# Two pads of 64 bytes that move every large on-chip tile of an encoder block from byte 64 to byte 0 modulo 128

## The chip, the cores and the metric

The kernel runs on one core of one Trainium2 chip. The metric is the device time of one execution in microseconds; of the kernel before, three runs are given, and their median counts.

## The reference, cut to what matters

One block of a streaming encoder works on x of 512 x 1024 in fp32. One input projection feeds two attention branches and their gates; each branch is projected, gated and summed, and an output projection and a layer norm follow. A gated MLP with a causal convolution of width 3 and a second layer norm end the block.

```
proj = x @ w_in                              # 1024 -> q/k/v of two branches, indexer, two gates
y_a  = top-k attention with a relative bias  # 8 heads of 64
y_s  = stick-breaking attention              # 8 heads of 64
merged = sigmoid(g_a + b_a) * (y_a @ w_branch_dsa) + sigmoid(g_b + b_b) * (y_s @ w_branch_sb)
x = layer_norm(alpha * x + merged @ w_out)
u, g = split(x @ w_ffn_in)                   # 1024 -> 2 x 2816
h = gelu(causal_dwconv(u, conv_w, conv_b)) * g
x = layer_norm(alpha * x + h @ w_ffn_out)    # 2816 -> 1024
```

## The kernel before, in words

Every product of fp32 operands is made of three matmuls (type fp32r): each operand is split into a high part, which ScalarE (ACT) writes with a copy, and a low part, which VectorE (DVE) or GpSimd (POOL) gets by subtracting the high part. The three are high x high, high x low and low x high. In the input projection (L233 to L235, and L270 to L272 for the values), the branch projections (L611 to L613, L817 to L819), the output projection (L866 to L868) and the MLP (L937 to L939, and L1017 to L1019 for its second half) the moving operand has 512 columns in most matmuls, 384 or 256 in some, and the stationary one is a 128 x 128 block. The second MLP product follows a Strassen scheme, with sums of weight blocks and of hidden blocks made on the way.

A stream object (class `Stream`) brings the weights in pieces of 128 x 1024: a DMA on the queue of SyncE (SP) fills a `raw` tile, L104 makes `whi` of it, L113 makes `wlo`, or for some pieces a negated copy (L107) and an accumulating DMA (L110) do. Three `raw`, three `whi` and three `wlo` buffers turn over. Attention heads run one after the other on ACT, DVE and POOL, and the list `FILL` names projections whose matmuls TensorE (PE) runs in between, a few at a time. The weights of the sticks or of the softmax are turned over for the last product of a head, by PE for the first heads (L452) and, for the later ones, by a pair of 16-bit DMA transposes from `own`, a view into the tile `bm` or `keep`, to `pl` (L478); `weigh` (L511) multiplies them with the values, and reads 128-column pieces with a gap between them, up to three in one matmul.

Where the tiles lie is set by pools. The pool `cst` opens first on the left side of SBUF (on-chip memory, 229,376 bytes in each of 128 partitions), behind 16,512 bytes that the program reserves. Its five tiles are one after the other, each taken up to a multiple of 32 bytes: `ident` (512 bytes in a partition), `mhalf` (4), `bgt` (16 fp32, the gate biases), `cwt` (22 x 4 fp32, the taps and biases of the convolution) and `wi` (24 fp32, padded to 32). The pools `rawp`, `ring`, `bp` and later `cp`, `tp`, `ep`, `fp`, `hp`, `rp` stand behind it on the left. On the right side the pool `edge` opens first, ending at byte 229,344, with one tile `rb` of 8 fp32; `xp`, and later `dp`, `qp`, `wp`, grow from it towards the left. All other small tiles go through the helper `padded`, which allots the free size rounded up to 32 fp32 and returns the part that was asked for:

```
def padded(pool, shape, dt=F32, **kw):
    n = int(np.prod(shape[1:]))
    t = pool.tile([shape[0], -(-n // 32) * 32], dt, **kw)[:, :n]
    return t if len(shape) == 2 else t.rearrange("p (a b) -> p a b", a=shape[1])
```

So every tile that lies behind `cst` or before `edge` has a size that is a multiple of 128 bytes, and all of them have one residue modulo 128: 64 on both sides. The first `raw` tile is at byte 17,600, the pool `bp` begins at 54,464, `x1h` is at 170,688, `xh` at 155,584. Of the tiles larger than 4 bytes in a partition `ident` alone begins at byte 0 modulo 128, at 16,512.

`bgt` is read as a per-partition bias, one column at a time, by the gates' activations (L639, L645, L799), and is filled by one DMA; `rb` is written on L669 and L670 and read by two small matmuls on L674.

Of the kernel before, what the change touches and what calls it, by code (L numbers as in the profile page):

```python
# [11 lines left out]
F32 = mybir.dt.float32  # L12
F32R = mybir.dt.float32r
# [8 lines left out]
H = 8  # L22
# [105 lines left out]
def tile_block(ctx: ExitStack, tc: tile.TileContext, xT, xN, w_qi, w_ki, w_t, w_v, w_br, w_o, w_fi, w_fo,  # L128
# [10 lines left out]
# [6 lines that stand above are left out]
    cst = ctx.enter_context(tc.tile_pool(name="cst", bufs=1))  # L145
    edge = ctx.enter_context(tc.tile_pool(name="edge", bufs=1, side="right"))
# [73 lines left out]
    nc.gpsimd.memset(mhalf, -0.5)  # L220
    nc.scalar.activation(mhalf, mhalf, AF.Sigmoid)
    nc.gpsimd.memset(mhalf, -0.5)
    bgt = cst.tile([128, 16], F32, name="bgt")
    cwt = cst.tile([128, FC, 4], F32, name="cwt")


# [437 lines left out]
    idx_keys()  # L664

    oh = bp.tile([64, NREL], F32R, tag="beta", bufs=2, name="oh")
    rb = edge.tile([64, H], F32R, name="rb")
    nc.gpsimd.tensor_copy(oh, ohf)
    nc.vector.tensor_copy(rb[0:32], rbf)  # L669
    nc.vector.tensor_sub(rb[32:64], rbf, r32(rb[0:32]))  # L670
# [628 lines left out]
```

## Time and profile before

| | |
|---|---|
| Time, median of 3 runs | 746.8 us (746.47 to 747.76) |
| Profiled execution, first to last instruction | 744.9 us, granted TensorE clock 0.998 |
| PE busy | 735.6 us, 99% |
| DVE busy | 572.0 us, 77% |
| ACT busy | 408.0 us, 55% |
| POOL busy | 148.8 us, 20% |
| DMA traffic | 117.03 MB |

The profiled execution gives its span, and no time of its own beside it: the span lies 1.9 us below the median of the runs, and that is taken as what lies around it.

Engines are PE (TensorE's matmuls), PEld (its weight loads), DVE, ACT, POOL and SP; an engine's name with a q is its instruction queue. "L104" is a line of the kernel. A group's row gives line, engine, operation, output<-inputs by the program's names, the tile's shape, the count, the total of busy us and the mean ns of one, and then the idle time in front of them. A row of the timeline gives start and length in us. Matmuls are pipelined, and the trace gives each its whole passage, so that rows of 0.39 us start every 0.23 us: the step from start to start is what a matmul costs.

### The profile page before, as it was taken

The page shows a single profiled execution, that of the slowest core. Times are in us where ns is not written, and L with a number is a line of the kernel's source. Part 1 is how long each engine was busy: PE and PEld are TensorE (multiplying, and loading weights), DVE is VectorE, ACT ScalarE, POOL GpSimd, SP SyncE. Part 2 cuts the span into 40 slices and gives each one's busy share as a digit, 9 for nine tenths or more (in the row PEclk, how much of TensorE's full clock was granted, in tenths as well). Part 3 has the DMA queues.
Part 4 walks back from the last instruction along what each step waited for, and adds up shares of the span by engine and source line. Part 5 has one row for each costly group of instructions (what it writes and reads, how often), then busy time and mean ns, then how long its engine had stood idle before and what let it go on. Part 6 is the DMA issues. An engine that isn't in the chain of part 4 may idle for free.

```text
span 744.9 us, 9755 instructions
## 1 busy us (share of the span) xinstructions
PE 735.6 (99%) x3477; PEld 616.9 (83%) x3477; DVE 572.0 (77%) x907; ACT 408.0 (55%) x572; POOL 148.8 (20%) x161
## 2 busy tenths in 40 slices
PE   9999999999999999999999999999999999999995
PEld 7888888888888888888889888888888888888885
DVE  5569888999679898668755866686767668668985
ACT  6466867797785587845473533443444344345430
POOL 0002224365743332000101111011101101110011
PEclk9999999999999999999999999999999999999999
DMA  7445887796476455527832544444443444448632
GB/s 266 157 128 188 207 172 173 158 214 163 116 181 154 135 126 136 131 85 247 289 57 86 170 141 142 141 143 143 141 166 114 161 136 149 144 140 268 202 130 84
DMA packets 73631, 117.03 MB, mean 157 GB/s; under 512 B 42536, under 2 KB 42792, under 8 KB 73584
## 3 DMA queue, kind: packets, MB, share of 16 engines
q1 hardware_dynamic: 66304, 93.98, 42.0%
q0 software_dynamic: 5744, 18.38, 9.9%
q10 hardware_dynamic: 1536, 4.06, 2.1%
q8 instruction: 27, 0.44, 0.3%
q14 instruction: 20, 0.16, 0.1%
HBM read 95.93 MB, written 9.98 MB: 142 GB/s over the span
## 4 chain that ended last, share of the span: by engine, by line
PE 89%; DVE 3%; POOL 2%; issue 2%; DMA 2%; ACT 2%; DVEq 0%; POOLq 0%; ACTq 0%
PE u_ps L937 5%; PE u_ps L939 5%; PE g_ps L937 5%; PE u_ps L938 5%; PE g_ps L939 5%; PE g_ps L938 5%; PE m L1019 2%; PE m L1017 2%; PE m L1018 2%; PE av_ps L511 2%; PE ga_ps L234 2%; PE ga_ps L233 2%; PE gb_ps L235 2%; PE gb_ps L234 2%; PE ga_ps L235 2%; PE gb_ps L233 2%
## 5 line engine op out<-in xcount | busy, mean ns | idle before, releaser
L104 ACT ACTIVATE whi<-raw 128x1024 fp32r<-128x1024 f32 (+1 forms) x124 | 123.8, 1001 | 143.1 <-PE g_ps L938 43.7
L113 DVE TENSOR_TENSOR wlo<-raw,whi 128x1024 fp32r<-128x1024 f32 (+1 forms) x105 | 123.9, 1181 | 36.3 <-ACT whi L104 35.6
L939 PE MATMUL u_ps<-x1h,wlo 128*128 128x512 f32 (+1 forms) x192 | 71.4, 372 | 0.0
L937 PE MATMUL u_ps<-x1h,whi 128*128 128x512 f32 (+1 forms) x192 | 71.3, 372 | 0.0
L938 PE MATMUL u_ps<-x1l,whi 128*128 128x512 f32 (+1 forms) x192 | 71.3, 371 | 0.0
L937 PE MATMUL g_ps<-x1h,whi 128*128 128x512 f32 (+1 forms) x184 | 69.9, 380 | 0.0
L938 PE MATMUL g_ps<-x1l,whi 128*128 128x512 f32 (+1 forms) x184 | 69.9, 380 | 0.0
L939 PE MATMUL g_ps<-x1h,wlo 128*128 128x512 f32 (+1 forms) x184 | 69.9, 380 | 0.0
L939 PEld LDWEIGHTS u_ps<-x1h,wlo 128*128 128x128 f32 x192 | 36.2, 188 | 6.3
L938 PEld LDWEIGHTS u_ps<-x1l,whi 128*128 128x128 f32 x192 | 36.2, 188 | 6.3
L937 PEld LDWEIGHTS u_ps<-x1h,whi 128*128 128x128 f32 x192 | 36.2, 188 | 6.2
L939 PEld LDWEIGHTS g_ps<-x1h,wlo 128*128 128x128 f32 x184 | 34.6, 188 | 6.6
L938 PEld LDWEIGHTS g_ps<-x1l,whi 128*128 128x128 f32 x184 | 34.6, 188 | 6.5
L937 PEld LDWEIGHTS g_ps<-x1h,whi 128*128 128x128 f32 x184 | 34.6, 188 | 6.5
L960 DVE TENSOR_TENSOR t<-raw 128x512 f32<-128x512 f32 x11 | 7.6, 693 | 40.1 <-DMA raw<-in_w_fo_dram 39.2
L569 POOL TENSOR_TENSOR bm<-win,score 128x256 f32<-128x256 f32 (+2 forms) x24 | 26.9, 1147 | 32.2 <-DMA pl<-bm 27.3
L985 ACT ACTIVATE c<-c,cwt 128x512 f32<-128x512 f32 x22 | 15.9, 725 | 27.5 <-DVE c L984 27.3
L979 POOL MEMSET u<- 128x2 f32 x22 | 2.1, 98 | 143.7 <-ACT whi L104 99.2
L993 DVE TENSOR_TENSOR hF<-g_ps,c 128x512 f32<-128x512 f32 x22 | 15.1, 687 | 19.7 <-PE g_ps L939 19.7
L835 POOL TENSOR_TENSOR rstd<-rstd,mhalf 128x1 f32<-128x1 f32 x8 | 7.7, 959 | 104.6 <-DVE rstd L834 104.6
L423 DVE MAX8 m<-score 128x8 f32<-128x256 f32 (+2 forms) x48 | 26.6, 556 | 0.9
L557 POOL TENSOR_TENSOR beta<-beta,keep 128x1280 f32<-128x1280 f32 x8 | 21.6, 2704 | 26.7 <-DVE keep L554 26.7
(576 smaller groups left out, 2088.3 us busy)
## 6 DMA issues: line engine op xcount, KB each, us to landing
raw<-in_w_fi_dram SPq DMA_DIRECT2D x44, 512.0 KB, 3.3
raw<-in_w_t_dram SPq DMA_DIRECT2D x32, 512.0 KB, 3.7
raw<-in_w_fo_dram SPq DMA_DIRECT2D x26, 512.0 KB, 4.2
wlo<-in_w_t_dram POOLq DMA_DIRECT2D x14, 512.0 KB, 5.8
raw<-in_w_br_dram SPq DMA_DIRECT2D x8, 512.0 KB, 4.0
raw<-in_w_o_dram SPq DMA_DIRECT2D x8, 512.0 KB, 4.1
raw<-in_w_v_dram SPq DMA_DIRECT2D x7, 512.0 KB, 4.6
raw_b<-in_w_fo_dram SPq DMA_DIRECT2D x6, 512.0 KB, 5.5
```

Of the source, the lines that this page charges most:

```text
L104: self.high = nc.scalar.activation(hi[:, :w], t[:, :w], AF.Copy).ins
L113: self.done[key] = eng.tensor_sub(lo[:, :w], t[:, :w], r32(hi[:, :w])).ins
L233: nc.tensor.matmul(ps[:M], wh[:, c], xh[k], start=(k == 0), stop=False)
L234: nc.tensor.matmul(ps[:M], wh[:, c], xl[k], start=False, stop=False)
L235: nc.tensor.matmul(ps[:M], wl[:, c], xh[k], start=False, stop=(k == KC - 1))
L423: nc.vector.max(m8, sc)
L557: nc.gpsimd.tensor_mul(beta, beta, keep[:, 1:ATT + 1])
L569: nc.gpsimd.tensor_add(bm[:, OFF[j]:OFF[j] + N], win[:, 512 - N:512], score[j])
L937: nc.tensor.matmul(ps[:, c], wh[:, kc], x1h[:, k, c], start=(k == 0), stop=False)
L938: nc.tensor.matmul(ps[:, c], wh[:, kc], x1l[:, k, c], start=False, stop=False)
L939: nc.tensor.matmul(ps[:, c], wl[:, kc], x1h[:, k, c], start=False, stop=(k == KC - 1))
L985: nc.scalar.activation(c, c, AF.Gelu_apprx_tanh, bias=cwt[:, f, 3:4])
```

## The change

```
-    bgt = cst.tile([128, 16], F32, name="bgt")
+    bgt = padded(cst, [128, 16], name="bgt")
...
-    rb = edge.tile([64, H], F32R, name="rb")
+    rb = edge.tile([64, 3 * H], F32R, name="rb")[:, :H]
```

`bgt` takes 128 bytes of a partition in place of 64, and `rb` takes 96 in place of 32; the columns that are used, and every instruction's operands apart from their addresses, stay. On the left, `cwt` moves from byte 96 to byte 32 modulo 128, and `wi` and everything behind it moves up by 64 bytes, the first `raw` tile to 17,664 (138 x 128). On the right everything before `rb` moves down by 64, `x1h` to 170,624 (1333 x 128). The narrowest space between a left and a right tile of one time, 256 bytes between `hp` and `qp`, becomes 128; no pair of tiles comes to share a byte that did not share one before.

## The prediction

> **What bounds the kernel now.** I read the page's first part, the chain that ended last, the busy time by stage, and then the starts of single matmuls.
>
> ```profile
> span 744.9 us, 9755 instructions
> PE 735.6 (99%) x3477; PEld 616.9 (83%) x3477; DVE 572.0 (77%) x907; ACT 408.0 (55%) x572; POOL 148.8 (20%) x161
> ...
> PE 89%; DVE 3%; POOL 2%; issue 2%; DMA 2%; ACT 2%; DVEq 0%; POOLq 0%; ACTq 0%
> ```
>
> The kernel is one stream of matmuls, and 89% of the chain is PE. The stages say where PE is whole (us, then busy us and instructions of each engine):
>
> ```profile
> 4.50:45.00 40.50, 40.23 (x200) 34.17 (x200) 24.31 (x36) 21.47 (x34) 0.71 (x1) 1.00 0.60 198
> 45.00:190.00 145.00, 145.00 (x706) 122.67 (x707) 130.54 (x265) 109.76 (x177) 56.79 (x44) 1.00 0.76 177
> 190.00:255.00 65.00, 64.66 (x307) 53.96 (x306) 53.93 (x89) 43.92 (x69) 30.33 (x26) 1.00 0.59 145
> 255.00:400.00 145.00, 145.00 (x709) 122.98 (x708) 111.08 (x176) 93.00 (x124) 17.18 (x21) 1.00 0.52 151
> 400.00:676.00 276.00, 276.00 (x1255) 230.06 (x1255) 194.69 (x259) 114.80 (x143) 35.91 (x53) 1.00 0.43 143
> 676.00:733.00 57.00, 57.00 (x267) 47.77 (x266) 48.50 (x67) 22.60 (x26) 4.17 (x6) 1.00 0.56 185
> ```
>
> PE shows no idle time to speak of, but its rows overlap and can cover small gaps, so I take what a matmul costs from start to start. First the chain in the MLP:
>
> ```profile
> 449.02 0.45 PE Q L1019 x2
> ...
> 474.86 0.45 PE Q L1019 x2
> ```
>
> Between these two stand one round of two hidden blocks: 2 x 48 matmuls of L937 to L939 and 18 of L1017 to L1019, 114 of 512 columns in 25.84 us, 226.67 ns each. Then 256 and 384 columns, from the timeline and the chain:
>
> ```profile
> 399.82 0.28 PE L939 MATMUL u_ps<-x1h,wlo 128*128 128x256 f32 x1
> ...
> 402.94 0.28 PE L937 MATMUL u_ps<-x1h,whi 128*128 128x256 f32 x1
> ```
>
> ```profile
> 10.16 0.52 PE qi_ps L312 x3
> ```
>
> With the 25 rows between, 26 steps of 256 columns take 3.12 us, 120.0 ns each; 384 columns take 0.52/3 = 173.3. The three lie on one line: 106.67 ns per 256 columns, and 13.33 ns a matmul on top. Those 13.33 ns are as long as 32 columns, and 32 columns of fp32 are 128 bytes. That is the one number in the profile that could speak for the change, so most of what follows is about it.
>
> Over the whole stream the columns (2847 matmuls of 512, 290 of 256, 200 of 384, 137 of 128, 3 of 8, counted in the trace) and 13.33 ns for each of the 3477 come to 723.8 us. The first start and the last are these:
>
> ```profile
> 1.20 2.99 PE L210 MATMUL idle_ps<-idle 128*128 128x512 bf16 x7 [1.20 <-DVE idle L207]
> ```
>
> ```profile
> 737.10 0.28 PE L1019 MATMUL m<-whi,bl 128*128 128x256 f32 x1
> ```
>
> That is 735.9 us, so 12.1 us are stalls: by the same subtraction 1.7 in the warm-up matmuls, 1.1 to 45 us, 4.5 to 190, 2.4 to 255, 2.1 to 320, and 0.4 in all the rest. Behind the last start lie 7.8 us of the last block's norm and output. Whatever does not change the 13.33 ns can win at most the 10 us of stalls behind the warm-up and a part of the 7.8.
>
> **The change part by part.** No instruction is added, removed or moved; no wait is added, since no pair of tiles comes to overlap that did not, and nothing is moved past a queue. The DMA that fills `bgt` and the copies into `rb` have the same shapes. What remains is the address, and it reaches three kinds of work.
>
> *Matmuls.* If a misaligned start made the 13.33 ns, each misaligned start should cost. `weigh` offers the test: its first moving operand is three runs of 128 columns with gaps, each run beginning at byte 64 modulo 128, and the same count of columns stands in one run elsewhere.
>
> ```profile
> 283.86 0.34 PE L511 MATMUL av_ps<-pth,va 128*128 128x384 f32 x1
> 284.04 0.34 PE L511 MATMUL av_ps<-ptl,va 128*128 128x384 f32 x1
> 284.21 0.22 PE L511 MATMUL av_ps<-pth,va 128*128 128x128 f32 x1
> ```
>
> Two matmuls of three runs take 0.35 us, 175 ns each, beside 173.3 for one run. Two more starts at byte 64 cost 1.7 ns, 0.8 each, which is within the 10 ns to which the rows are given; by the theory they would cost 26.7. The second witness is the warm-up row above: its moving tile, of bf16, is at 54,464, byte 64 modulo 128 too, and 7 matmuls take 2.99 us, 427 ns each. At half the column rate found above, 512 columns are 426.7 ns, and nothing is left for a start. So the 13.33 ns belong to the fp32 matmul, not to its address, as far as these rows reach. I take 0. Both ends for the range, from the nearest row: 0.8 ns on each of 3477 starts, 2.9 us less or more.
>
> [...]
>
> *DVE, ACT and POOL.* The convolution reads the same tile at offsets of 4 and 8 bytes, and the norm reads tiles at their beginning; output, width and operation agree.
>
> ```profile
> L983 DVE SCALAR_TENSOR_TENSOR c<-u,cwt,c x22: 743/750/1401, 406.8 to 670.1; 128x512 f32<-128x512 f32 x22
> ```
>
> ```profile
> L984 DVE SCALAR_TENSOR_TENSOR c<-u,cwt,c x22: 739/752/753, 408.6 to 671.9; 128x512 f32<-128x512 f32 x22
> ```
>
> ```profile
> L839 DVE SCALAR_TENSOR_TENSOR r<-r,mv,ln 128x512 f32<-128x512 f32 x14 | 9.8, 746 | 0.0
> ...
> L980 ACT ACTIVATE u<-u_ps 128x512 f32<-128x512 f32 x22 | 12.8, 581 | 0.0
> L1155 ACT ACTIVATE m<-P 128x512 f32<-128x512 f32 x2 | 1.1, 583 | 0.0
> ```
>
> Offsets 4, 8 and 0 give 750, 752 and 746 ns; on ACT a copy from PSUM to offset 8 takes 581 and one to offset 0 takes 583. An engine's time moves by 0.8% at most with the address. I take 0; DVE, ACT and POOL carry 7% of the chain, 52 us, so the bound is 0.4 us either way. Where these engines lie beside PE, its matmuls cover them: 130.5 us of DVE against 145.0 of PE in the tightest stage, and DVE would have to slow by 11% to lose that cover.
>
> *DMA.* All weight loads now land at another byte of a row. In a stretch that is DMA alone (355 to 360 us):
>
> ```profile
> DMA packets 580, 2.08 MB, mean 416 GB/s; under 512 B 72, under 2 KB 72, under 8 KB 580
> ...
> q1 hardware_dynamic: 559, 2.03, 100.2%
> ```
>
> The queue moves 2.03 MB, 496 packets of 4 KB, in 100.2% of 16 x 5 us: 162 ns a packet, 10.1 for 256 bytes. [...]
>
> *The sum.* 0 for PE, 0 for the engines, -0.1 for DMA: the profiled execution stays at 744.8, and with the 1.9 us between span and median the time is 746.7 us. A difference under 0.2%, 1.5 us, cannot be told from no change here: the three runs spread over 1.3 us.
>
> **The rivals.**
>
> *Faster, by PE:* the beginning of a moving operand is fetched only when the matmul before has ended, a 128-byte piece at a time, and a start in its middle wastes half or all of the 13.33 ns; later runs are fetched ahead, so that the three-run row is blind to it. For it: 13.33 ns is just 128 bytes. Against: the bf16 row, and 175 beside 173.3. Price: behind 255 us PE is alone, and 2231 matmuls (709, 1255 and the 267 of the last stretch) save 29.7 us; of the 1213 before, 16.2 us, DVE's 130.5 of 145 us leaves perhaps half. Together 38, so 709 us if all of it goes, 728 if half.
>
> [...] The transposes move packets of 256 bytes from `own`, which goes from byte 192 to byte 0 modulo 256. In one of them:
>
> ```profile
> DMA packets 2489, 0.62 MB, mean 175 GB/s; under 512 B 2489, under 2 KB 2489, under 8 KB 2489
> ...
> q1 hardware_dynamic: 2489, 0.62, 93.4%
> ```
>
> 93.4% of 16 x 3.55 us over 2489 packets is 21.3 ns for 256 bytes, where a 4 KB packet takes 10.1 ns for as many. [...]
>
> *Slower, by a transpose that lands late:* loads that end a little earlier let SP issue the next one earlier, and it meets a transpose. The piece of 5.88 us lies beside two loads:
>
> ```profile
> raw<-in_w_t_dram SPq DMA_DIRECT2D x1, 512.0 KB, 4.3
> win<-s_win SPq DMA_DIRECT2D x1, 256.0 KB, 4.1
> pl<-bm SPq DMA_TRANSPOSE x1, 5.9
> ```
>
> The piece of 3.55 us is alone until its last half us, 2.3 us shorter. A second such meeting on the chain, in the heads between 190 and 320 us where PE waits already, adds 2.3 us: 749.1 us. It decides when the fillers in front of the head last less than those 2.3 us; PE's 64.66 of 65.00 busy us says that they just last now.
>
> *It doesn't do what it says:* a pad could be undone by the allocator's own rounding, or the residues could have been equal already. Against it stand the sizes: 512 + 32 + 64 + 352 + 128 behind byte 16,512 is 17,600, 64 over 137 x 128, and the new 64 bytes end at 138 x 128. The time would be 746.8.
>
> **How the numbers follow.** No change: 0.72, as two witnesses speak against the only large term. It doesn't do what it says: 0.02, and also no change. PE faster: 0.12, because 13.33 ns fit 128 bytes too well and no row here has an aligned fp32 operand to compare. Transposes: 0.06. A late transpose: 0.08. That gives faster 0.18, same 0.74, slower 0.08. The range takes the forecast with its bounds (0.8 ns a start, 0.4 and 0.9 us, of which not all fall to one side), reaches down to the transposes' 744.6 and a little on, and up to the late transpose's 749.1: 744.0 to 749.2. It leaves out the gain on PE, and the rare sums of bounds.
>
> **What would show it.** Right: steps of 226.67, 120.0 and 173.3 ns as before, L983, L984, L839 and L980 at the means shown, and stalls near 12 us. PE's rival: MLP rounds of 114 matmuls under 25.84 us. [...] The prediction is wrong if a matmul's fixed part moves by more than 0.5 ns (1.7 us in all), or if stalls grow or shrink by over 1.5 us.

## The result, and the profile after

The changed kernel takes 757.98 us (median of 4 runs, 757.44 to 758.07) where the kernel before takes 746.77 (746.47 to 747.76): a ratio of 1.0145 [1.0131, 1.016], 11.2 us slower. The forecast was 746.7, and 749.2 was the upper end of its range. Every engine runs the same instructions in the same order as before.

From the page of the changed kernel: its span, its engines, and its chain.

```profile
span 756.3 us, 9755 instructions
...
PE 747.5 (99%) x3477; PEld 618.6 (82%) x3477; DVE 571.6 (76%) x907; ACT 409.0 (54%) x572; POOL 149.2 (20%) x161
...
PE 98%; DVE 1%; issue 0%; DVEq 0%
```

The span is 11.4 us longer, and PE is busy 11.9 us longer; DVE, ACT and POOL differ by 1.0 us at most. The busy time by stage of the same kernel (us, then busy us and instructions of PE, PEld, DVE, ACT and POOL, and PE's granted clock) shows it in another way:

```profile
45.00:190.00 145.00, 145.00 (x700) 120.92 (x699) 129.42 (x262) 108.42 (x174) 54.30 (x42) 1.00 0.76 178
...
255.00:400.00 145.00, 145.00 (x684) 121.32 (x683) 110.56 (x177) 92.61 (x122) 19.16 (x19) 1.00 0.48 146
400.00:676.00 276.00, 276.00 (x1245) 225.56 (x1244) 191.12 (x252) 111.26 (x139) 36.69 (x56) 1.00 0.41 139
```

PE is full in these stages, at the full clock, as before, but gets through 700, 684 and 1245 matmuls in place of 706, 709 and 1255. So a matmul has become dearer, and that is what the steps from start to start say. The changed kernel's chain in the MLP:

```profile
454.35 0.45 PE Q L1019 x2
...
480.83 0.45 PE Q L1019 x2
```

The round of 114 matmuls takes 26.48 us, not 25.84. Of the 114, 96 are those of L937 to L939, with a moving operand (`x1h`, `x1l`) from the right side of SBUF and a stationary one (`whi`, `wlo`) from the left. If these alone pay, it is 0.64/96 = 6.7 ns each. (Every one of the eight full rounds of a kernel has the same length within 2 ns, before and after.) The changed kernel's timeline of PE there (start, length):

```profile
508.07 0.40 PE L937 MATMUL g_ps<-x1h,whi 128*128 128x512 f32 x1
508.30 0.39 PE L938 MATMUL g_ps<-x1l,whi 128*128 128x512 f32 x1
508.52 0.40 PE L939 MATMUL g_ps<-x1h,wlo 128*128 128x512 f32 x1
508.76 0.39 PE L937 MATMUL g_ps<-x1h,whi 128*128 128x512 f32 x1
...
510.86 0.40 PE L937 MATMUL g_ps<-x1h,whi 128*128 128x512 f32 x1
```

Twelve steps in 2.79 us are 232.5 ns each, where 226.67 stood before, and the rows alternate between 0.39 and 0.40 us. With 256 columns (the same kernel's timeline) nothing has changed:

```profile
395.25 0.28 PE L937 MATMUL u_ps<-x1h,whi 128*128 128x256 f32 x1
...
401.01 0.28 PE L937 MATMUL u_ps<-x1h,whi 128*128 128x256 f32 x1
```

48 steps in 5.76 us, 120.0 ns each. The groups by line and form show which 512-column matmuls pay. The mean of their overlapping rows carries the same sign:

```profile
L937 PE MATMUL u_ps<-x1h,whi 128*128 128x512 f32 x160 | 63.2, 395 | 0.0
...
L234 PE MATMUL gb_ps<-xl,whi 128*128 128x512 f32 x64 | 25.4, 397 | 0.0
...
L1017 PE MATMUL Q<-whi,ah 128*128 128x512 f32 x22 | 8.6, 389 | 0.0
```

Before, these were 389, 392 and 389. `Q`, whose two operands both lie on the left, has not moved.

As the order is the same, the two traces can be subtracted step by step. From the first matmul's start to the last one's it is 735.90 us before and 747.22 after, 11.32 more. The tail behind is 7.8 and 7.9. Sorted by line, for 512 columns:

| lines | operands | matmuls | mean step before, after (ns) | sum (us) |
|---|---|---|---|---|
| L937 to L939 | right moving, left stationary | 984 | 226.7, 233.3 | +6.45 |
| L233 to L235 | right moving, left stationary | 771 | 229.0, 233.4 | +3.36 |
| L270 to L272 | left moving, right stationary | 192 | 230.2, 233.1 | +0.54 |
| L817 to L819 | right moving, left stationary | 96 | 228.0, 232.9 | +0.47 |
| L866 to L868 | both on one side | 192 | 226.7, 226.7 | 0.00 |

L233 to L235 have 21 more, of a projection (`ki`) whose weight blocks are 72 columns wide and so begin at other bytes. The 2194 steps of 512 columns whose operands lie on two sides, and began at the same byte modulo 256 before, give +11.53 us, if four with a wait in the trace before are left out (with them +10.67): 5.3 ns each. The 607 fp32 steps whose operands lie on one side give +0.09. The rest of the 11.32 is mostly in five longer waits behind steps of 384 columns at the start (+0.77). The cost is in the pairs that cross from one side to the other.

### The profile page after: what moved, and what is told of

Its sections match the earlier page's. It is cut to its first block, busy times and chain, and to the rows that moved or that the text cites. A ratio compares the mean times of both kernels' runs of the same rounds, so it can differ in the third digit from the quotient of the medians.

```text
span 756.3 us, 9755 instructions
## 1 busy us (share of the span) xinstructions
PE 747.5 (99%) x3477; PEld 618.6 (82%) x3477; DVE 571.6 (76%) x907; ACT 409.0 (54%) x572; POOL 149.2 (20%) x161
## 3 DMA queue, kind: packets, MB, share of 16 engines
q1 hardware_dynamic: 66304, 93.98, 40.7%
## 4 chain that ended last, share of the span: by engine, by line
PE 98%; DVE 1%; issue 0%; DVEq 0%
PE u_ps L939 5%; PE u_ps L938 5%; PE u_ps L937 5%; PE g_ps L939 5%; PE g_ps L937 5%; PE g_ps L938 5%; PE av_ps L511 3%; PE m L1018 2%; PE m L1017 2%; PE m L1019 2%; PE ga_ps L234 2%; PE ga_ps L233 2%; PE gb_ps L233 2%; PE gb_ps L234 2%; PE gb_ps L235 2%; PE ga_ps L235 2%
## 5 line engine op out<-in xcount | busy, mean ns | idle before, releaser
L113 DVE TENSOR_TENSOR wlo<-raw,whi 128x1024 fp32r<-128x1024 f32 (+1 forms) x105 | 122.2, 1166 | 38.7 <-ACT whi L104 38.1
L939 PE MATMUL u_ps<-x1h,wlo 128*128 128x512 f32 (+1 forms) x192 | 72.3, 377 | 0.0
L937 PE MATMUL u_ps<-x1h,whi 128*128 128x512 f32 (+1 forms) x192 | 72.2, 376 | 0.0
L938 PE MATMUL u_ps<-x1l,whi 128*128 128x512 f32 (+1 forms) x192 | 72.2, 376 | 0.0
L939 PE MATMUL g_ps<-x1h,wlo 128*128 128x512 f32 (+1 forms) x184 | 70.9, 385 | 0.0
L937 PE MATMUL g_ps<-x1h,whi 128*128 128x512 f32 (+1 forms) x184 | 70.8, 385 | 0.0
L938 PE MATMUL g_ps<-x1l,whi 128*128 128x512 f32 (+1 forms) x184 | 70.8, 385 | 0.0
L937 PEld LDWEIGHTS u_ps<-x1h,whi 128*128 128x128 f32 x192 | 36.1, 188 | 7.3
L938 PEld LDWEIGHTS u_ps<-x1l,whi 128*128 128x128 f32 x192 | 36.1, 188 | 7.3
L939 PEld LDWEIGHTS u_ps<-x1h,wlo 128*128 128x128 f32 x192 | 36.1, 188 | 7.3
L939 PEld LDWEIGHTS g_ps<-x1h,wlo 128*128 128x128 f32 x184 | 34.5, 188 | 7.6
L938 PEld LDWEIGHTS g_ps<-x1l,whi 128*128 128x128 f32 x184 | 34.5, 188 | 7.6
L937 PEld LDWEIGHTS g_ps<-x1h,whi 128*128 128x128 f32 x184 | 34.6, 188 | 7.5
```

Of the source, the lines that this page charges most:

```text
L113: self.done[key] = eng.tensor_sub(lo[:, :w], t[:, :w], r32(hi[:, :w])).ins
L937: nc.tensor.matmul(ps[:, c], wh[:, kc], x1h[:, k, c], start=(k == 0), stop=False)
L938: nc.tensor.matmul(ps[:, c], wh[:, kc], x1l[:, k, c], start=False, stop=False)
L939: nc.tensor.matmul(ps[:, c], wl[:, kc], x1h[:, k, c], start=False, stop=(k == KC - 1))
```

## The experiments

The theory formed from these rows: the pads move left tiles up by 64 bytes and right tiles down by 64, so two operands that stood at the same byte modulo 256 (192 and 192) now stand 128 bytes apart (0 and 128). What counts is this **distance**, moving address less stationary address, modulo 256. The rivals: one side's own byte counts (the stationary operand at 0, or the moving one at 128); or the byte modulo 128 does.

**Four placements that tell distance from place.** The first pads the left side alone, the second the right alone, the third both, so that all is at byte 0 modulo 256, and the fourth the right by 128 bytes, so that all stays at byte 64 modulo 128 and the sides come apart by 128.

```
left_only      bgt = cst.tile([128, 32], F32, name="bgt")[:, :16]
right_only     rb = edge.tile([64, 3 * H], F32R, name="rb")[:, :H]
both_0_of_256  bgt as in left_only, and rb = edge.tile([64, 7 * H], ...)[:, :H]
apart_128      rb = edge.tile([64, 5 * H], F32R, name="rb")[:, :H]
```

> Only the pad of bgt: left tiles at byte 0, right tiles at byte 192 modulo 256, so that a right tile stands 192 bytes past a left one modulo 256 (0 in the kernel before, 128 in the changed one). Theory of the distance (what counts is how far the moving operand of a matmul and the stationary one that is loaded beside it stand apart modulo 256; 0 costs 226.7 ns for 512 columns, 128 costs 233.3): 192 is a distance that no run has shown; if the cost grows evenly with the distance, 230 ns in mixed matmuls and 752 us, and the same in the run with only the right pad. Theory of the place (a tile that begins at byte 128 modulo 256 is slow whatever the other does): no tile stands there, 746.8 us. Theory of the left side (it is the move of the left tiles or of cwt that costs): 758 us.

> Only the wider rb: left tiles at byte 192, right tiles at byte 128 modulo 256; the distance is 192 again. Theory of the distance: the same time as with the left pad alone, 752 us if the cost grows evenly. Theory of the place: the right tiles stand at 128, so mixed matmuls take 233.3 ns and the kernel 758 us. Theory of the left side: 746.8 us.

> The pad of bgt and rb of 7 x 8 columns (224 bytes): left and right tiles all at byte 0 modulo 256, distance 0. Theory of the distance: 226.7 ns in all matmuls of 512 columns and 746.8 us, as before the change. Theory of the place: 746.8 us too, since nothing stands at 128. Theory of the left side: 758 us. If alignment to 128 or 256 were bad in itself: 758 us.

> The kernel before with rb of 5 x 8 columns (160 bytes), bgt without its pad: left tiles at byte 192, right tiles at byte 64 modulo 256, so every tile keeps byte 64 modulo 128 as in the kernel before, but the distance is 128. Theory of the distance: 233.3 ns in mixed matmuls and 758 us, as in the changed kernel. Theory of the place (byte 128 modulo 256, or byte 0 modulo 128): 746.8 us. Theory of the left side: 746.8 us.

The kernel before ran at 747.17 us beside these. The round of 114 matmuls in the chain, first left_only, then right_only, both_0_of_256 and apart_128:

```profile
453.71 0.45 PE Q L1019 x2
...
480.21 0.45 PE Q L1019 x2
```

```profile
453.36 0.45 PE Q L1019 x2
...
479.86 0.45 PE Q L1019 x2
```

```profile
449.27 0.45 PE Q L1019 x2
...
475.11 0.45 PE Q L1019 x2
```

```profile
454.94 0.45 PE Q L1019 x2
...
481.42 0.45 PE Q L1019 x2
```

26.50, 26.50, 25.84 and 26.48 us. In whole times, left_only 758.4 (1.0141 [1.0126, 1.0156]), right_only 757.91 (1.0136 [1.0121, 1.0151]), both_0_of_256 746.78 (0.9991 [0.9982, 1.0001]) and apart_128 758.04 (1.0137 [1.012, 1.0154]). Either pad alone costs as much as both, and moving both sides to byte 0 costs nothing: no side's own byte is at fault. In apart_128 every large tile keeps its byte modulo 128 and the whole loss is there: the byte modulo 128 is out, and what counts goes by 256 or more. That it is 256 the kernel before shows: `raw` starts at 17,600 and its buffers are 4,096 bytes long, as are those of `whi` behind it, so the weights are at byte 192 modulo 512; `x1h` (170,688) is at 192 too, but `xh` (155,584) at 448. Yet the median step of 512 columns is 227 ns in the MLP and in the projections alike. Byte 0 and byte 192 are equally good: 25.84 us a round in both_0_of_256 and in the kernel before. The guess of a cost that grows evenly with the distance missed: it gave 752 us for a single pad.

**The curve by distance.** The pad of `rb` alone sets the distance in steps of 32 bytes. With H = 8, a tile of [64, n * H] puts it at 192, 128, 64, 32, 224, 96 and 160 for n = 3, 5, 7, 8, 2, 6 and 4.

```
dist_64   rb = edge.tile([64, 7 * H], F32R, name="rb")[:, :H]
dist_32   8 * H      dist_224  2 * H
dist_96   6 * H      dist_160  4 * H
```

> The kernel before with rb of 7 x 8 columns (224 bytes): left tiles at byte 192, right tiles at byte 0 modulo 256. Matmuls with a right moving operand and a left stationary one (some 1930 of 512 columns) have distance 64, the value projections, which have them the other way round (192), distance 192. In the two runs with one pad it was the other way: 192 for the many (233.3 ns), 64 for the value projections (229.3 ns). Theory of the signed distance (64 costs about 2.5 ns, 192 and 128 about 6.5, 0 nothing): 1930 x 2.5 and 192 x 6.5 ns, 6 us, so 753 us, with 229 to 230 ns in the MLP's first half. Rival, the kind of matmul (the value projections are cheaper at any distance that is not 0 or 128, the others not): 233.3 ns in the MLP's first half and 758 us.

> The kernel before with rb of 2 x 8 columns (64 bytes): left tiles at byte 192, right tiles at byte 160 modulo 256, distance 224 or -32. Theory that every distance but 0 costs, 64 less than the others: 233 ns and 757 to 758 us. Rival, that the distance counts in steps of 64 or 128 bytes and 32 is within one: 226.7 ns and 746.8 us. Between the two if the cost grows evenly from 0.

> The kernel before with rb of 8 x 8 columns (256 bytes): left tiles at byte 192, right tiles at byte 224 modulo 256, distance 32. Theory of a cost that grows with the distance ahead: about 228 ns and 750 us. Theory of steps: 226.7 ns and 746.8 us, or, if 32 falls into the next step, the 229 ns of distance 64 and 753 us.

> The kernel before with rb of 6 x 8 columns (192 bytes): right tiles at byte 32, left ones at byte 192 modulo 256, distance 96. Shown so far: 0 is free, 64 costs 2.5 ns, 32, 128, 192 and 224 about 6.5. Theory that 0 and 64 alone are special: 233 ns and 758 us. Rival, a cost that falls with the closeness to 64: 230 to 231 ns and 753 to 755 us.

> The kernel before with rb of 4 x 8 columns (128 bytes): right tiles at byte 96, left ones at byte 192 modulo 256, distance 160. Theory that 0 and 64 alone are special: 233 ns and 758 us. Rival, that the cost depends on the distance modulo 64 (0 at multiples of 64 being partly cheaper): slower than 128 and 192, as 32 and 224 were by 1 us, 759 us.

The rounds of dist_64, dist_32, dist_160, dist_96 and dist_224:

```profile
451.04 0.45 PE Q L1019 x2
...
477.16 0.45 PE Q L1019 x2
```

```profile
454.45 0.45 PE Q L1019 x2
...
480.97 0.45 PE Q L1019 x2
```

```profile
456.36 0.45 PE Q L1019 x2
...
482.94 0.45 PE Q L1019 x2
```

```profile
456.18 0.45 PE Q L1019 x2
...
482.71 0.45 PE Q L1019 x2
```

```profile
455.28 0.45 PE Q L1019 x2
...
481.79 0.45 PE Q L1019 x2
```

| distance | kernel | round (us) | over 25.84, per crossing matmul (ns) | time (us), ratio |
|---|---|---|---|---|
| 0 | both_0_of_256 | 25.84 | 0 | 746.78, 0.9991 [0.9982, 1.0001] |
| 32 | dist_32 | 26.52 | 7.1 | 759.45, 1.0164 [1.0149, 1.0179] |
| 64 | dist_64 | 26.12 | 2.9 | 751.53, 1.006 [1.0045, 1.0075] |
| 96 | dist_96 | 26.53 | 7.2 | 760.36, 1.0178 [1.0163, 1.0194] |
| 128 | apart_128 | 26.48 | 6.7 | 758.04, 1.0137 [1.012, 1.0154] |
| 160 | dist_160 | 26.58 | 7.7 | 760.96, 1.0183 [1.0169, 1.0197] |
| 192 | right_only | 26.50 | 6.9 | 757.91, 1.0136 [1.0121, 1.0151] |
| 224 | dist_224 | 26.51 | 7.0 | 759.05, 1.0158 [1.0141, 1.0175] |

The theories of an even growth and of steps of 64 or 128 bytes fall with 32 and 224, that of closeness to 64 with 96. The four distances that are not multiples of 64 take up to 3 us longer than 128 and 192, as the rival of dist_160 has it, but only 0.1 us or less in a round. Only 64 is cheaper than the rest, and it has a sign. The value projections (L270 to L272) move a left tile over a right one, so their distance is the negative of the others'. In left_only they have 64 while the rest have 192, and take 229.3 ns from start to start; in dist_64 they have 192 while the rest have 64, and take 232.9. So the cheap case is the moving operand 64 bytes above the stationary one, modulo 256, and not 64 below.

**The changed kernel with one moving operand moved back.** 128 more bytes in `x1l` put `x1h` and `x1l` at byte 0 modulo 256, beside weights at 0. The projections' operands stay as the change left them.

```
-    x1l = qp.tile([128, KC, S], F32R, name="x1l")
+    x1l = qp.tile([128, KC * S + 32], F32R, name="x1l")[:, :KC * S].rearrange("p (k t) -> p k t", k=KC)
```

> The changed kernel with 128 spare bytes behind x1l, so that x1h and x1l alone move down by 128 to byte 0 modulo 256, where the left tiles are; all other tiles stay as the change puts them. Theory of the distance: the 984 matmuls of 512 columns in the MLP's first half go from 233.3 to 226.7 ns, 6.5 us, and those of 384 and 512 columns in the input projection, the branches and the attention stay slow: 751.4 us. Theory that the address costs elsewhere (DMA landings, DVE, waits of the attention): 758 us.

It takes 751.5 us (751.11 to 752.4) beside 747.57. By line and form:

```profile
L937 PE MATMUL u_ps<-x1h,whi 128*128 128x512 f32 x160 | 62.2, 389 | 0.0
...
L234 PE MATMUL gb_ps<-xl,whi 128*128 128x512 f32 x64 | 25.4, 397 | 0.0
```

and its round in the chain:

```profile
453.65 0.45 PE Q L1019 x2
...
479.50 0.45 PE Q L1019 x2
```

The MLP is back at 25.85 us and 389 ns a row, the projection still has its 397: 6.5 us of the loss were the 984 matmuls of the MLP, and are gone with one tile's place.

**Which stationary operand: the one in use, or the one being loaded.** While a matmul streams, the weights of the next are loaded: in the changed kernel's timeline the load for an L938 begins at 508.07 us, together with the L937 ahead of it, and lasts 0.19 us of that matmul's 0.40. In lo_apart the sides are as before, but `wlo` alone has its own pool, 128 bytes apart from everything else. So L937 (here L943) has its own and the next weights at its own byte, L938 (L944) has a distance of 128 to the next weights, L939 (L945) to its own.

```
+    gap1, ring2 (bufs=3), gap2 = pools behind one another; gap1 and gap2 hold one [128, 32] tile each
-                lo = self.ring.tile([128, 1024], F32R, tag="wlo", name=f"wlo_{self.ns}")
+                lo = self.ring2.tile([128, 1024], F32R, tag="wlo", name=f"wlo_{self.ns}")
```

> The kernel before with 128 spare bytes ahead of the wlo buffers and 128 behind them: wlo at byte 64, whi and all other large tiles at the bytes of the kernel before modulo 256, the order of all instructions as before. In the projections and the MLP's first half the three matmuls of a step have the stationary operands whi, whi, wlo and the moving ones at byte 192. Theory of the load beside (a matmul's moving reads meet the load of the next matmul's stationary operand): the second of each three is slow, L234 and L938 at 233 ns, L233, L235, L937 and L939 at 226.7. Rival, the own operand (what counts is the distance to the stationary operand that the matmul itself uses): the third is slow, L235 and L939 at 233 ns. Both: some 640 of those and some 200 with a moving wlo, 6.5 ns each, 5.5 us, 752.3 us.

It takes 755.01 us (754.63 to 755.69), 1.0107 [1.0093, 1.0121]; either theory gave about 5.5 us, and it is 8.2. By line and form:

```profile
L945 PE MATMUL u_ps<-x1h,wlo 128*128 128x512 f32 x160 | 63.5, 397 | 0.0
...
L944 PE MATMUL u_ps<-x1l,whi 128*128 128x512 f32 x160 | 63.4, 396 | 0.0
L943 PE MATMUL u_ps<-x1h,whi 128*128 128x512 f32 x160 | 62.2, 389 | 0.0
```

```profile
L1024 PE MATMUL Q<-wlo,ah 128*128 128x512 f32 x22 | 8.7, 395 | 0.0
...
L1023 PE MATMUL Q<-whi,ah 128*128 128x512 f32 x22 | 8.5, 389 | 0.0
...
L1025 PE MATMUL Q<-whi,al 128*128 128x512 f32 x22 | 6.9, 388 | 0.0
```

From start to start L943 takes 226.8, L944 232.4 and L945 234.1 ns; in the second product, where `wlo` is the moving operand, L1024 alone is slow: 232.2 beside 226.6, and 234.0 for the 107 of its 143 whose `wlo` lies in the moved pool. Both theories fall as they stood: by these steps a matmul pays if its moving operand is apart from the weights in use or from those loaded next, and nearly as much for one (234.1 and 232.4 ns) as for both (233.3 in the changed kernel). The part of the next weights is shown by L944, whose own weights agree. That of the own weights is less sure, as L945 always follows a slow L944, and a cost can linger: in the changed kernel the first three steps of `P`, which follow the round's crossing matmuls, take 231, 233 and 231 ns before they come back to 227, though their operands agree. Against lingering speaks that the step behind L945 or L1024 is not slow (226.8 and 226.6 ns).

**The small pool `bp`.** In the kernel before, the attention tiles in `bp` are at byte 64 modulo 256, as `rbf` ahead of them is padded to 128 bytes only. A few steps there cross from a filler matmul at 192 to one of a head at 64. In the timeline of the kernel before:

```profile
271.12 0.39 PE L234 MATMUL ka_ps<-xl,whi 128*128 128x512 f32 x1
271.34 0.40 PE L235 MATMUL ka_ps<-xh,wlo 128*128 128x512 f32 x1
271.58 0.34 PE L511 MATMUL av_ps<-ptl,va 128*128 128x384 f32 x1
```

```
-    rbf = padded(bp, [32, H], name="rbf")
+    rbf = bp.tile([32, 8 * H], F32, name="rbf")[:, :H]
```

> The kernel before with rbf of 64 x 4 bytes in place of 128 bytes, so that the attention's tiles (keys, queries, values, turned weights) move from byte 64 to byte 192 modulo 256, where the weights and x are; instruction order as before. Theory of the distance: about 100 matmuls at the edges between projection and attention pieces, which now lie 128 apart, save up to 6 ns each, 0.6 us: 746.2 us, and no more than the measurement can just tell. Rival, that these edges cost for another reason: 746.8 us.

746.45 us (745.8 to 746.93, 11 runs) beside 746.8: 0.9993 [0.9984, 1.0002], not to be told from no change. The steps do fall: 51 of 512 columns from a filler into a head from 18.3 ns over their columns to 14.4, and 26 inside heads from 19.5 to 14.9, 0.3 us in all. The 26 had their own and the next weights at distance 0 in the kernel before too, so the rule of lo_apart does not cover them. 25 of them stand one to three steps behind a step that pays, as the first steps of `P` do; that the cost lingers there fits, but was not tried by itself. No version that ran beats the kernel before by what can be measured.

## Why the prediction was wrong, point by point

**The step that failed** is "Matmuls" in the part "The change part by part": the address was priced at 0, with 0.8 ns a start as its bound, on two witnesses of one operand's own byte. The question was put for one operand; the runs answer for two (758.4 us in left_only and 757.91 in right_only, 746.78 in both_0_of_256). Both witnesses were blind to that: `weigh` reads `pth` and `va` at the same byte modulo 256, distance 0, and the warm-up matmul takes both operands from one tile, and ran at half the column rate (427 ns for 512 columns), so that it tells nothing of a start at the full one. The fixed 13.33 ns are indeed not owed to the address, as said: at byte 0 they are the same (25.84 us in both_0_of_256). What the step left out is that the two pads move the sides apart, which the diff's own sentence tells: left up by 64, right down by 64. The missing term is 2190 crossing matmuls of 512 columns by 5.27 ns, 11.53 us, against 11.2 measured.

**The witness that was there.** The step from 271.34 to 271.58, above, is 0.24 us, where its neighbour is 0.22: 40 such steps, whose next weights lie 128 bytes off, have 18.7 ns over their columns, beside 14.0 for 2726 whose operands all agree. A step into other work looked like a short wait, and I did not sort steps by the addresses of both operands.

**The bound of 0.8 ns a start** was for that reason too small by a factor of 6.6, and the range ended 8.8 us below the result.

**DVE, ACT and POOL at 0** was right. By line and form, in the changed kernel:

```profile
L983 DVE SCALAR_TENSOR_TENSOR c<-u,cwt,c 128x512 f32<-128x512 f32 x22 | 17.1, 779 | 0.4
L984 DVE SCALAR_TENSOR_TENSOR c<-u,cwt,c 128x512 f32<-128x512 f32 x22 | 16.5, 751 | 0.7
...
L980 ACT ACTIVATE u<-u_ps 128x512 f32<-128x512 f32 x22 | 12.8, 581 | 0.0
L839 DVE SCALAR_TENSOR_TENSOR r<-r,mv,ln 128x512 f32<-128x512 f32 x14 | 9.8, 744 | 0.0
```

751, 581 and 744 ns stand beside 752, 581 and 746; the 779 is a mean with a single long instruction in it, as the 1401 ns was before.

**DMA at -0.1** is not contradicted: the DMA queues have no share in the changed kernel's chain, so no run shows this term by itself, nor the 0.9 us that the range has for DMA. The queue of the weights, first before, then after:

```profile
q1 hardware_dynamic: 66304, 93.98, 42.0%
```

```profile
q1 hardware_dynamic: 66304, 93.98, 40.7%
```

42.0% of 744.9 us and 40.7% of 756.3 are 312.9 and 307.8 us of 16 engines: no slower. No late transpose stands behind the loss.

**The transposes**, with 0.06 among the chances, moved their packets faster, though no gain shows in the time: no run shows the 744.6 us to which the range reaches down, and the least median of all kernels that ran is 746.45 us, in bp_same. A 256-byte packet of a transpose has a median of 18 ns in both kernels, but the mean tells more. The six transposes behind the first norm (`own` into `got`, L906) go from byte 192 to byte 0 modulo 256. One pair of them, before and after:

```profile
DMA packets 2111, 0.52 MB, mean 187 GB/s; under 512 B 2111, under 2 KB 2111, under 8 KB 2111
```

```profile
DMA packets 2110, 0.52 MB, mean 215 GB/s; under 512 B 2110, under 2 KB 2110, under 8 KB 2110
```

Over all six, a packet takes 21.6 ns in the mean before, with 16% over 25 ns, and 17.9 after, with none over 25. That is 17% less. In the heads only every other pair of transposes goes from byte 192 to 0, as the prediction has it for all: the two buffers of `bm` and `keep` lie 5,248 bytes apart, so the other pairs go from 64 to 128, and most of these stay at 21 to 22 ns. The changed kernel's chain has no DMA in it, so nothing there waited for these packets.

**Stalls near 12 us** was right: columns and 13.33 ns come to 723.8 us, with 11.53 more to 735.3, and the matmuls take 747.2, so 11.9 us are stalls. Yet PE's share of the chain rose from 89 to 98%. That share says which instruction was late last, not how much was lost.

**The rivals** had one that ended slower, but it was sought among waits and queues. The right one, that the pads put a matmul's two operands apart, was not among them.

## What to carry to other kernels

A pad that moves every tile has not done one thing but as many as there are pairs: for an instruction with two operands, sort its steps by the difference of the two addresses before pricing either address. On this kernel a 512-column fp32r matmul of the MLP took 226.7 ns with its moving operand at the same byte modulo 256 as its own weights and the next ones, and 233.3 at 128 bytes from both. Both at byte 0 modulo 128 was not enough (757.98 us), and byte 192 modulo 256 was as good as byte 0 (746.77 and 746.78 us). Where pools grow from both ends of the memory, a pad on one side moves that difference for every crossing pair: here 32 bytes on the right alone gave 759.05 us (dist_224).

## What the runs showed of the hardware that was not expected

- The distance costs 6.7 to 7.7 ns for 512 columns at 32, 96, 128, 160, 192 and 224 bytes, 2.9 ns at 64, nothing at 0. At 128 the steps come as 229 and 237 to 238 ns by turns.
- With 256 columns a distance of 128 costs nothing (120.0 ns in both kernels), with 384 it costs 1.5 ns (174.5 and 176.0 ns, 91 steps of L312 to L314 without a wait).
- The six transposes behind the first norm (L906) move their 256-byte packets in 17.9 ns in the mean when they read from byte 0 modulo 256, and in 21.6 from byte 192.
- In lo_apart L944, whose own weights are at its byte modulo 256 and only the next ones 128 bytes apart, takes 232.4 ns, and L943, with both at its byte, 226.8.
- Why a moving operand 64 bytes above is cheaper (2.9 ns), why the matmuls of 256 columns are spared, and why being apart from both weights (233.3 ns) costs no more than from one (232.4 and 234.1) was not tried further and stays open.
